# Seven-product tiles four tiles earlier in one feed-forward and two earlier in another, and scores with the other sign

## The chip, the cores and the metric

The kernel runs on one core of a Trainium2 chip. The metric is device time in microseconds (us) of one execution; lower is better. The core has a matrix engine (PE, with its weight loads shown as PEld), three engines for elementwise work (DVE, ACT, POOL) and one that issues the transfers (SP). Each has a queue of its own; they meet through semaphores.

## The reference

A two-layer decoder trunk on 1024 positions of width 1024, all in float32.

- Layer 0: a causal convolution module (norm, 1024 to 2048 matmul, gating, a depthwise convolution of 31 taps, layer norm, silu, 1024 to 1024 matmul) added to the stream, then a feed-forward.
- Then keys and values for three attention branches (compressed, selected, window) are projected once.
- Layer 1: attention of 16 heads over the three branches, gated and summed, then a feed-forward. A final norm ends it.

```
gate, up = split(rmsnorm(x) @ w_in)          # 1024 -> 2 x 2816
x = x + (silu(gate) * up) @ w_out            # 2816 -> 1024
s = where(valid, (q . k) * scale - slope * dist, -1e30);   p = softmax(s)
```

With 1024 positions and 16 blocks of 64, every block is selected, so the selected branch is full causal attention.

## The kernel before

**Staging.** Columns are positions; the 1024 positions are two halves of 512 (c = 0, 1). The kernel does layer 0 for half 0, then half 1 behind it, and so on; there are four feed-forwards, called as `ffn(layer, half)` in the order (0,0), (0,1), (1,0), (1,1). While the first runs, the convolution and the layer norm of half 1 run beside it. While (0,1) and (1,0) run, the attention of a half runs beside them. The last one, (1,1), has the final norm of half 0 beside it.

**Precision.** Each float32 operand is split into a high part (ACT copies it to fp32r) and a low part (the rest, a subtraction on DVE or POOL), and a product is three matmuls: high by high, high by low, low by high.

**A feed-forward** has 22 hidden tiles of 128 rows, j = 0 to 21 (tile 8 is the ninth). In a plain tile (`ffn_gu`) the gate and the up product are 8 blocks x 3 = 24 matmuls of 512 columns each, 48 in all (L137). After them DVE multiplies gate by up (L583), ACT takes the high part (L592) and DVE the low part (L593). After some tiles PE does a part of the second product, "the outs": 8 output tiles, each a sum over a few hidden tiles, added to the stream by DVE (L606). Which tiles go together is in `PARTS`; for (0,0) the parts start at tiles 0, 4, 8, 12, 16, 19, and the outs of a part come right after the first tile of the next.

**A seven-product tile** (`ffn_gu7`, `weights7`, `mm7`) does the 2x2 block product of (gate, up) by (first, second 256 columns) with seven block products in place of eight: 7 x 4 blocks x 3 = 84 matmuls of 256 columns (L507). `mm7` runs the products in the order 1, 2, 6, 5, 7, 3, 4. Its operands need sums:

- of the weights, for each tile: four sums on DVE (L479 to L482), seven high parts on ACT (L491), five low parts on POOL and two on DVE (L492);
- of the results: L522, L526, L527, L531 and two gating products, L561 and L562, on DVE;
- of the activations, once per feed-forward (`blocks7`, `blocks`): four groups k = 0 to 3. Each has two adds (L286), two subtractions on DVE (L439, L440) and two on POOL (L441, L442), two high parts on ACT (L452) and a low part on DVE and one on POOL (L453). Products 5 and 6 read the DVE half, products 7 and 4 the POOL half, products 1, 2 and 3 the plain activations. Every product runs over all four groups.

`ffn` takes `seven`, the first tile that is done so: `N7 = 12` for (0,0), `NREG = 4` for (1,1); the other two have none. The groups are emitted behind earlier tiles:

```
for j in range(*p):
    yield from (self.ffn_gu7 if j >= seven else self.ffn_gu)(l, j, c)
    if seven < FT and seven - 3 <= j < seven:
        self.mark(self.last)
        next(y7, None)
        next(y7, None)
```

Each `next` makes one group. `mark` and `later` hold the adds of a group (L286) in DVE's queue behind the last instruction of tile j (L593). So groups 0 and 1 stand behind tile max(seven - 3, 0), groups 2 and 3 behind the next tile.

**What sets the order.** PE's order is the order of the program text. A background generator (the convolution, the attention) is advanced by a rate per microsecond of PE work. DVE, ACT, POOL and SP get their order at build time from a list scheduler with its own time model, within data and buffer dependences. On the chip each queue runs in that order.

**The background of (0,0)**, for each of 8 tiles: DVE does 21 taps (L322, L332), POOL 9 (L329), DVE joins them (L336) and adds to a running sum (L343). Then PE spreads the sum (L382), DVE centres (8 x L385), ACT squares and DVE adds seven times (L190); PE sums that (L201), DVE takes the root, PE spreads it (L220).

**The scores** (`scores`): PE makes q.k, a DVE instruction adds the distance term and keeps the row maximum (L987), DVE negates the maximum (L993), ACT takes exp with it as bias and sums the row (L995), DVE inverts the sum (L997), POOL scales (L1000). The distance table is written once (`bias_base`); q is scaled in `q_tile`.

Of the kernel before, what the change touches and what calls it, by code (L numbers as in the profile page):

```python
# [22 lines left out]
AF = mybir.ActivationFunctionType  # L23
OP = mybir.AluOpType
# [7 lines left out]
HG = 8  # L32
DH = 64
# [1 line left out]
FH = 2816  # L35
FT = FH // 128
EPS = 1e-6
NEG = -1e30
LC = 32
NCMP = 63  # L40
SLC0 = 64
# [14 lines left out]
        (1, 0): (4, 8, 12, 15, 18), (1, 1): (4, 8, 12, 16, 19)}  # L56
PARTS = {k: list(zip((0,) + v, v + (FT,))) for k, v in CUTS.items()}
RSTD1 = 4.0
N7 = 12
PRE = 1  # L60
RAWB = (1, 2)
LNP = (), (1, 4, 6)
# [14 lines left out]
SLOPE = [2.0 ** (-8.0 * (h + 1) / NH) for h in range(NH)]  # L77
# [12 lines left out]
PP = 4  # L90
YE = 23
WX = 3
NREG = 4
FIN0 = 60.0
H = T // 2
WB = 4
# [6 lines left out]
class Net:  # L103
# [724 lines left out]
    def q_tile(self, j, c):  # L828
        nc = self.nc
        w = self.wload(self.wq[j], 8)  # L830
        ps = self.mm_ps()
        yield from self.mm3(ps, w, self.y[c], range(KT))
        for g in range(2):
            a = slice(g * DH, (g + 1) * DH)
            b = slice((1 - g) * DH, (2 - g) * DH)
            f = DH ** -0.5 / SLOPE[g * HG + j]
            q = self.tmp("q", F32R)
            nc.scalar.activation(q[a], ps[a], AF.Copy, scale=f)
            nc.vector.scalar_tensor_tensor(q[b], ps[a], f, q[a].bitcast(F32),
                                           OP.mult, OP.subtract)  # L840
            qd = self.dram.tile([128, T], F32, name=f"qd{g}_{j}_{c}")
            nc.sync.dma_start(qd, q.bitcast(F32))
            self.qd[g, j, c] = qd
# [58 lines left out]
    def bias_base(self):  # L902

        nc = self.nc
        b = self.base
        for (c0, w, step, off) in ((0, S, 1, 896), (BT_WIN, 640, 1, 512),
                                   (BT_CMP, 119, 16, 896 - (LC - 1))):
            nc.gpsimd.iota(b[:, c0:c0 + w], pattern=[[step, w]], base=-off,
                           channel_multiplier=-1, allow_small_or_imprecise_dtypes=True)
            nc.gpsimd.affine_select(out=b[:, c0:c0 + w], in_=b[:, c0:c0 + w],  # L910
                                    pattern=[[-step, w]], compare_op=OP.is_ge, fill=NEG,
                                    base=off, channel_multiplier=1)
        nc.gpsimd.affine_select(out=b[:, BT_WIN:BT_WIN + 640], in_=b[:, BT_WIN:BT_WIN + 640],
                                pattern=[[1, 640]], compare_op=OP.is_ge, fill=NEG,
                                base=-1, channel_multiplier=-1)

    def load_group(self, c, g):
# [31 lines left out]
    def scores(self, out, K, q, g, head, i, win):  # L949


        nc = self.nc
        ql = (i % 4) * 128
        mx = self.sm.tile([128, 8], F32, name="mx", tag="mx", bufs=10)
        sm = self.sm.tile([128, 2], F32, name="sm", tag="sm", bufs=10)
        if win:
            n = 128 * min(i + 1, 5)
            P = self.Pp.tile([128, 640], F32, name="PW", tag="PW", bufs=6)
            key0 = 128 * max(i - 4, 0)
            segs = [(2, 0, n, BT_WIN + 128 * max(4 - i, 0))]  # L960
        else:
            nv = NCMP if i >= 4 else NCMP // 2
            n = 64 + 128 * (i + 1)
            P = self.Pp.tile([128, 64 + S], F32, name="PS", tag="PS", bufs=5)
            key0 = 0
            segs = [(0, 0, nv, BT_CMP + 8 * (7 - i)), (1, 64, n - 64, 128 * (7 - i))]
        out[i] = P
        m = -(-n // T)
        w = -(-n // (m * 32)) * 32
        prev, spare = {}, 2  # L970
        for a in range(m):
            k0, k1 = a * w, min((a + 1) * w, n)
            ps = self.psc.tile([128, T], F32, name="sc", tag="sc", bufs=3)
            for e, k in enumerate(K[win]):
                nc.tensor.matmul(ps[:, :k1 - k0], q[:, ql:ql + 128], k[:, key0 + k0:key0 + k1],  # L975
                                 start=e == 0, stop=e == 1)
            for e, (br, p0, pn, b0) in enumerate(segs):
                s0, s1 = max(p0, k0), min(p0 + pn, k1)
                if s0 >= s1:
                    continue  # L980
                col = e
                if s1 < p0 + pn:
                    col = spare
                    spare += 1
                init = mx[:, prev[e]:prev[e] + 1] if e in prev else -3.0e38
                prev[e] = col
                nc.vector.tensor_tensor_reduce(  # L987
                    P[:, s0:s1], ps[:, s0 - k0:s1 - k0], self.base[:, b0 + s0 - p0:b0 + s1 - p0],
                    SLOPE[head], init, OP.add, OP.max, mx[:, col:col + 1])
            if a < m - 1:  # L990
                yield 2 * MM * (k1 - k0) / T
        ns = len(segs)
        nc.vector.tensor_scalar(mx[:, :ns], mx[:, :ns], -1.0, None, OP.mult)  # L993
        for e, (br, p0, pn, b0) in enumerate(segs):
            nc.scalar.activation(P[:, p0:p0 + pn], P[:, p0:p0 + pn], AF.Exp,  # L995
                                 bias=mx[:, e:e + 1], accum_out=sm[:, e:e + 1])
        nc.vector.reciprocal(sm[:, :ns], sm[:, :ns])  # L997
        for e, (br, p0, pn, b0) in enumerate(segs):
            gt = br * NH + head
            nc.gpsimd.tensor_scalar(P[:, p0:p0 + pn], P[:, p0:p0 + pn], sm[:, e:e + 1],  # L1000
                                    self.gates[:, i, gt:gt + 1], OP.mult, OP.mult)
        yield 2 * MM * (k1 - k0) / T
# [201 lines left out]
    def go(self, main, time=1e9):  # L1204


        if main is None:
            return False
        while time > 0:
            x = next(main, None)  # L1210
            if x is None:
                return False
            time -= x
            if self.bg is not None:
                self.owed += x * self.rate
                while self.owed > 0:
                    y = next(self.bg, None)
                    if y is None:
                        self.bg = None
                        break  # L1220
                    self.owed -= y
        return True
# [11 lines left out]
    def run(self):  # L1234
# [144 lines left out]
        go(fill)  # L1379
        go(self.ffn(0, 0, N7, True))  # L1380
        self.rest()
# [95 lines left out]
        self.silu = True  # L1477
        g = self.ffn(1, 1, NREG, True)
        go(g, FIN0)
# [62 lines left out]
```

## Time and profile before

| | |
|---|---|
| median of 3 runs | 2625.26 us (2624.68 to 2629.07) |
| the profiled execution | 2629.18 us |
| its span, first to last instruction | 2627.5 us |
| instructions | 37191 |
| PE busy | 2512.0 us (96%) |
| DVE busy | 1765.8 us (67%) |
| POOL busy | 1469.2 us (56%) |
| ACT busy | 1291.6 us (49%) |

The profile lists each instruction with its line, its engine, its tiles and its start; idle time in front of an instruction is put down to what released it. Matmuls overlap in the listing: the distance between two starts is what one costs. The stretches that matter here are 380 to 510 us (the first feed-forward with the convolution of half 1 beside it), 850 to 1345 and 1500 to 2150 us (the two attentions), and 2237 us to the end (the last feed-forward).

### The profile page before, as it was taken

The page shows a single profiled execution, that of the slowest core. Times are in us where ns is not written, and L with a number is a line of the kernel's source. Part 1 is how long each engine was busy: PE and PEld are TensorE (multiplying, and loading weights), DVE is VectorE, ACT ScalarE, POOL GpSimd, SP SyncE. Part 2 cuts the span into 40 slices and gives each one's busy share as a digit, 9 for nine tenths or more (in the row PEclk, how much of TensorE's full clock was granted, in tenths as well). Part 3 has the DMA queues.
Part 4 walks back from the last instruction along what each step waited for, and adds up shares of the span by engine and source line. Part 5 has one row for each costly group of instructions (what it writes and reads, how often), then busy time and mean ns, then how long its engine had stood idle before and what let it go on. Part 6 is the DMA issues. An engine that isn't in the chain of part 4 may idle for free. (4 is left out here: it accounts for less than half of the span.)

```text
span 2627.5 us, 37191 instructions
## 1 busy us (share of the span) xinstructions
PE 2512.0 (96%) x12946; PEld 2083.5 (79%) x12946; DVE 1765.8 (67%) x3652; ACT 1291.6 (49%) x2517; POOL 1469.2 (56%) x1156
## 2 busy tenths in 40 slices
PE   8898899999799999999999999999999999899997
PEld 6676788888677878887878788888888887698986
DVE  6995788677774556665556566667666655777775
ACT  6555554444534554555543355555555543334444
POOL 8794889666543554555543354535445433566664
PEclk9999899999899999999999999999999999999999
DMA  4222223232446222322355531213212124143332
GB/s 163 72 73 66 80 81 97 88 93 92 152 146 190 87 89 62 112 86 82 90 161 167 190 101 45 81 44 108 70 53 74 54 78 158 58 129 97 97 95 75
DMA packets 111212, 258.29 MB, mean 98 GB/s; under 512 B 17265, under 2 KB 28848, under 8 KB 111024
## 3 DMA queue, kind: packets, MB, share of 16 engines
q1 hardware_dynamic: 111024, 255.91, 31.0%
q8 instruction: 102, 1.67, 0.3%
q14 instruction: 86, 0.70, 0.1%
HBM read 226.37 MB, written 29.42 MB: 97 GB/s over the span
## 5 line engine op out<-in xcount | busy, mean ns | idle before, releaser
L160 POOL TENSOR_TENSOR wl<-wr,wh 128x1024 fp32r<-128x1024 f32 (+2 forms) x396 | 740.6, 1872 | 661.1 <-ACT wh L158 625.1
L137 PE MATMUL mm<-yh,wh 128*128 128x512 f32 x1424 | 595.4, 418 | 31.7 <-DVE yl L179 30.4
L137 PE MATMUL mm<-yl,wh 128*128 128x512 f32 x1424 | 567.6, 399 | 5.0 <-DVE yl L179 5.0
L137 PE MATMUL mm<-yh,wl 128*128 128x512 f32 x1424 | 566.2, 398 | 1.8 <-POOL wl L160 1.8
L158 ACT ACTIVATE wh<-wr 128x1024 fp32r<-128x1024 f32 (+2 forms) x396 | 332.5, 840 | 426.3 <-PE mm L137 287.1
L137 PE MATMUL mm<-gh,wh 128*128 128x512 f32 x1360 | 439.4, 404 | 1.8 <-ACT gh L592 1.4
L137 PEld LDWEIGHTS mm<-yh,wh 128*128 128x128 f32 x1424 | 272.1, 191 | 86.3 <-DVE yl L179 32.1
L137 PEld LDWEIGHTS mm<-yh,wl 128*128 128x128 f32 x1424 | 271.3, 191 | 63.5 <-POOL wl L160 2.2
L137 PEld LDWEIGHTS mm<-yl,wh 128*128 128x128 f32 x1424 | 272.6, 191 | 49.5 <-DVE yl L179 6.2
L1030 DVE TENSOR_TENSOR pl<-pt,ph 128x512 fp32r<-128x512 f32 (+3 forms) x320 | 206.4, 646 | 149.6 <-ACT ph L1029 148.7
L137 PEld LDWEIGHTS mm<-gh,wh 128*128 128x128 f32 x1360 | 243.3, 189 | 48.8 <-issue 3.5
L137 PE MATMUL mm<-gh,wl 128*128 128x512 f32 x680 | 270.0, 397 | 3.7 <-POOL wl L160 3.7
L1029 ACT ACTIVATE ph<-pt 128x512 fp32r<-128x512 f32 (+3 forms) x320 | 178.7, 559 | 177.6 <-PE pt L1026 175.2
L1000 POOL TENSOR_SCALAR PS<-PS,sm,gates 128x31 f32<-128x31 f32 (+9 forms) x256 | 154.7, 615 | 191.4 <-DVE sm L997 164.6
L332 DVE SCALAR_TENSOR_TENSOR mm<-u,vec,mm 128x512 f32<-128x512 f32 x306 | 225.6, 752 | 8.0 <-PE mm L320 1.8
L995 ACT ACTIVATE PS<-PS,mx 128x31 f32<-128x31 f32 (+9 forms) x256 | 139.5, 546 | 115.6 <-DVE mx L993 115.3
L329 POOL TENSOR_TENSOR zb<-zb,cv 128x512 f32<-128x512 f32 x132 | 178.8, 1355 | 14.4 <-ACT zb L314 8.8
L1000 POOL TENSOR_SCALAR PW<-PW,sm,gates 128x640 f32<-128x640 f32 (+4 forms) x128 | 96.2, 752 | 155.1 <-DVE sm L997 131.8
L606 DVE TENSOR_TENSOR h<-mm,h 128x512 f32<-128x512 f32 x184 | 124.7, 684 | 81.7 <-PE mm L137 81.3
L137 PEld LDWEIGHTS mm<-gh,wl 128*128 128x128 f32 x680 | 128.0, 188 | 37.7 <-POOL wl L160 7.5
L995 ACT ACTIVATE PW<-PW,mx 128x640 f32<-128x640 f32 (+4 forms) x128 | 88.8, 694 | 101.2 <-DVE mx L993 100.5
L507 PE MATMUL mm<-y,wh 128*128 128x256 f32 x1008 | 133.8, 286 | 2.3 <-DVE wh L492 1.9
(243 smaller groups left out, 4814.4 us busy)
## 6 DMA issues: line engine op xcount, KB each, us to landing
wr<-in_fin_dram SPq DMA_DIRECT2D x176, 512.0 KB, 3.3
wr<-in_fout_dram SPq DMA_DIRECT2D x128, 256.0 KB, 2.7
wr<-in_pw_dram SPq DMA_DIRECT2D x46, 512.0 KB, 3.3
wr<-in_fout_dram SPq DMA_DIRECT2D x64, 192.0 KB, 2.4
wr<-in_wq_dram SPq DMA_DIRECT2D x16, 512.0 KB, 4.0
qd<-q SPq DMA_DIRECT2D x32, 256.0 KB, 2.2
qt<-qd SPq DMA_DIRECT2D x32, 256.0 KB, 2.8
wr<-in_wo_dram SPq DMA_DIRECT2D x16, 512.0 KB, 3.7
```

Source lines behind the costliest of these rows:

```text
L137: nc.tensor.matmul(ps, x[:, a, :], y_, start=start and a + b == 0, stop=stop and a == n - 1 and b == 2)
L158: nc.scalar.activation(wh[:, :kt, :cols], wr[:, :kt, :cols], AF.Copy)
L160: e.tensor_tensor(wl[:, :kt, :cols], wr[:, :kt, :cols], wh[:, :kt, :cols].bitcast(F32), OP.subtract)
L329: nc.gpsimd.tensor_tensor(zb, zb, t, OP.add)
L332: later(nc.vector.scalar_tensor_tensor(ps, u[:, w:w + T], dw(w), ps, OP.mult, OP.add))
L507: nc.tensor.matmul(ps, u[:, a], v, start=a + b == 0, stop=a == n - 1 and b == 2)
L606: self.nc.vector.tensor_tensor(h, ps, h, OP.add)
L995: nc.scalar.activation(P[:, p0:p0 + pn], P[:, p0:p0 + pn], AF.Exp, bias=mx[:, e:e + 1], accum_out=sm[:, e:e + 1])
L1000: nc.gpsimd.tensor_scalar(P[:, p0:p0 + pn], P[:, p0:p0 + pn], sm[:, e:e + 1], self.gates[:, i, gt:gt + 1], OP.mult, OP.mult)
L1029: nc.scalar.activation(ph[:rows, :width], pt[:rows, :width], AF.Copy)
L1030: nc.vector.tensor_tensor(pl[:rows, :width], pt[:rows, :width], ph[:rows, :width].bitcast(F32), OP.subtract)
```

## The change

Two constants and one sign.

- `N7` goes from 12 to 8: in (0,0) tiles 8 to 11 become seven-product tiles; groups 0 and 1 now stand behind tile 5, groups 2 and 3 behind tile 6.
- `NREG` goes from 4 to 2: in (1,1) tiles 2 and 3 become seven-product tiles; groups 0 and 1 stand behind tile 0, groups 2 and 3 behind tile 1.
- q is scaled with the other sign, the distance table has the other sign, the row maximum becomes a row minimum, exp gets scale -1, and the 256 negations (L993) are gone. An added empty line moves the line numbers from there on by one, until the removed line moves them back.

```
-NEG = -1e30
+FAR = 1e30
-N7 = 12
+N7 = 8
-NREG = 4
+NREG = 2
...
-            f = DH ** -0.5 / SLOPE[g * HG + j]
+            f = -DH ** -0.5 / SLOPE[g * HG + j]
...
-            nc.gpsimd.iota(b[:, c0:c0 + w], pattern=[[step, w]], base=-off,
-                           channel_multiplier=-1, allow_small_or_imprecise_dtypes=True)
+            nc.gpsimd.iota(b[:, c0:c0 + w], pattern=[[-step, w]], base=off,
+                           channel_multiplier=1, allow_small_or_imprecise_dtypes=True)
...
-                init = mx[:, prev[e]:prev[e] + 1] if e in prev else -3.0e38
+                init = mx[:, prev[e]:prev[e] + 1] if e in prev else 3.0e38
...
-                    SLOPE[head], init, OP.add, OP.max, mx[:, col:col + 1])
+                    SLOPE[head], init, OP.add, OP.min, mx[:, col:col + 1])
...
-        nc.vector.tensor_scalar(mx[:, :ns], mx[:, :ns], -1.0, None, OP.mult)
...
-            nc.scalar.activation(P[:, p0:p0 + pn], P[:, p0:p0 + pn], AF.Exp,
+            nc.scalar.activation(P[:, p0:p0 + pn], P[:, p0:p0 + pn], AF.Exp, scale=-1.0,
                                  bias=mx[:, e:e + 1], accum_out=sm[:, e:e + 1])
```

PE's order is the same in both programs but for the converted tiles and the place of the background's few matmuls among them.

**DVE in the last feed-forward**, before, around the last group and the first seven-product tile (`wh` and `ws` are weights, `et`, `y` the activation sums, `g`, `gh` the hidden tile, `u` the first result of a seven-product tile):

```order
L440 TENSOR_TENSOR et<-yt,et 128x256
L480 TENSOR_TENSOR ws<-ws,wr 128x512
L481 TENSOR_TENSOR ws<-wr 128x512
L453 TENSOR_TENSOR y_22231<-et,y_22230 128x512
L439 TENSOR_TENSOR et<-yt 128x256
L440 TENSOR_TENSOR et<-yt,et 128x256
L482 TENSOR_TENSOR ws<-wr,ws 128x512
L453 TENSOR_TENSOR y_22249<-et,y_22248 128x512
L583 SCALAR_TENSOR_TENSOR mm<-mm,sg 128x512
L492 TENSOR_TENSOR wh<-wr,wh 128x512
L593 TENSOR_TENSOR gh<-mm,gh 128x512
L522 TENSOR_TENSOR u<-mm,et 128x512
```

and after the change:

```order
L583 SCALAR_TENSOR_TENSOR mm<-mm,sg 128x512
L492 TENSOR_TENSOR wh<-wr,wh 128x512
L593 TENSOR_TENSOR gh<-mm,gh 128x512
L286 TENSOR_TENSOR yt<-yh,yl 128x512 x4
L439 TENSOR_TENSOR et<-yt 128x256
L440 TENSOR_TENSOR et<-yt,et 128x256
L453 TENSOR_TENSOR y_22186<-et,y_22185 128x512
L439 TENSOR_TENSOR et<-yt 128x256
L440 TENSOR_TENSOR et<-yt,et 128x256
L479 TENSOR_TENSOR ws<-wr 128x512
L453 TENSOR_TENSOR y_22204<-et,y_22203 128x512
L522 TENSOR_TENSOR u<-mm,et 128x512
```

Before, the low part of group 3 (the second L453) is followed by the end of a whole plain tile (L583, L593) ahead of the first seven-product result (L522). After, the last plain tile (L583, L593) stands ahead of groups 2 and 3, and L522 right behind them.

**DVE in the first feed-forward**, before, around the end of the convolution and its centring (`z`, `acc`: the convolution; `h`: the outs):

```order
L332 SCALAR_TENSOR_TENSOR mm<-u,vec,mm 128x512 x2
L606 TENSOR_TENSOR h_94<-mm,h_94 128x512
L332 SCALAR_TENSOR_TENSOR mm<-u,vec,mm 128x512
L606 TENSOR_TENSOR h_95<-mm,h_95 128x512
L606 TENSOR_TENSOR h_96<-mm,h_96 128x512
L606 TENSOR_TENSOR h_97<-mm,h_97 128x512
L336 TENSOR_TENSOR z<-mm,zb 128x512
L343 TENSOR_TENSOR acc<-acc,z 128x512
L606 TENSOR_TENSOR h_98<-mm,h_98 128x512
L606 TENSOR_TENSOR h_99<-mm,h_99 128x512
L606 TENSOR_TENSOR h_100<-mm,h_100 128x512
L385 SCALAR_TENSOR_TENSOR z<-mm,z 128x512 x8
```

and after:

```order
L593 TENSOR_TENSOR gh<-et,gh 128x512
L336 TENSOR_TENSOR z<-mm,zb 128x512
L482 TENSOR_TENSOR ws<-wr,ws 128x512
L606 TENSOR_TENSOR h_99<-mm,h_99 128x512
L479 TENSOR_TENSOR ws<-wr 128x512
L343 TENSOR_TENSOR acc<-acc,z 128x512
L606 TENSOR_TENSOR h_100<-mm,h_100 128x512
L492 TENSOR_TENSOR wh<-wr,wh 128x512
L480 TENSOR_TENSOR ws<-ws,wr 128x512
L481 TENSOR_TENSOR ws<-wr 128x512
L385 SCALAR_TENSOR_TENSOR z<-mm,z 128x512 x8
L482 TENSOR_TENSOR ws<-wr,ws 128x512
```

Before, only outs (L606) stand around the last steps of the convolution (L336, L343). After, weight sums and low parts of seven-product tiles (L479 to L482, L492) stand between them and behind them, ahead of the centring (L385).

**DVE in the first feed-forward, groups 2 and 3**: before,

```order
L286 TENSOR_TENSOR yt<-yh,yl 128x512 x2
L439 TENSOR_TENSOR et<-yt 128x256
L286 TENSOR_TENSOR yt<-yh,yl 128x512
L440 TENSOR_TENSOR et<-yt,et 128x256
L286 TENSOR_TENSOR yt<-yh,yl 128x512
L453 TENSOR_TENSOR y_4004<-et,y_4003 128x512
L439 TENSOR_TENSOR et<-yt 128x256
L440 TENSOR_TENSOR et<-yt,et 128x256
L453 TENSOR_TENSOR y_4022<-et,y_4021 128x512
L583 SCALAR_TENSOR_TENSOR mm<-mm,sg 128x512
```

and after:

```order
L439 TENSOR_TENSOR et<-yt 128x256
L332 SCALAR_TENSOR_TENSOR mm<-u,vec,mm 128x512
L440 TENSOR_TENSOR et<-yt,et 128x256
L332 SCALAR_TENSOR_TENSOR mm<-u,vec,mm 128x512 x2
L453 TENSOR_TENSOR y_3451<-et,y_3450 128x512
L286 TENSOR_TENSOR yt<-yh,yl 128x512
L332 SCALAR_TENSOR_TENSOR mm<-u,vec,mm 128x512
L286 TENSOR_TENSOR yt<-yh,yl 128x512
L439 TENSOR_TENSOR et<-yt 128x256
L440 TENSOR_TENSOR et<-yt,et 128x256
L583 SCALAR_TENSOR_TENSOR mm<-mm,sg 128x512
L453 TENSOR_TENSOR y_3469<-et,y_3468 128x512
```

Before, the groups follow each other with no taps between; after, convolution taps (L332) stand between their steps, and the end of tile 7 (L583) ahead of the last low part.

## Rows read from the trace of the kernel before

**Rows 1.** Page, busy us, share of the span and instructions of each engine.
```profile
PE 2512.0 (96%) x12946; PEld 2083.5 (79%) x12946; DVE 1765.8 (67%) x3652; ACT 1291.6 (49%) x2517; POOL 1469.2 (56%) x1156
```

**Rows 2.** Windows; busy us (count) of PE, PEld, DVE, ACT, POOL, granted clock, DMA share, GB/s.
```profile
400.00:450.00 50.00, 50.00 (x221) 41.20 (x220) 45.78 (x63) 27.23 (x40) 47.12 (x33) 1.00 0.26 80
408.36:476.46 68.10, 68.10 (x297) 55.51 (x296) 56.72 (x75) 35.17 (x52) 57.54 (x38) 1.00 0.31 97
530.99:575.50 44.51, 42.38 (x338) 40.75 (x337) 38.29 (x47) 19.80 (x40) 29.57 (x21) 1.00 0.29 90
2328.72:2369.00 40.28, 40.28 (x339) 40.23 (x338) 34.31 (x47) 18.03 (x36) 26.99 (x17) 1.00 0.33 110
```

**Rows 3.** Timeline of PE, first feed-forward; start, us, engine, line, operation [idle <-releaser].
```profile
440.72 0.63 PE L137 MATMUL mm<-gh,wh 128*128 128x512 f32 x2
...
463.14 1.02 PE L382 MATMUL mm<-acc,ones 128*128 128x512 f32 x2
...
479.23 0.28 PE L201 MATMUL mm<-ones,acc 128*128 128x1 f32 x2
...
498.54 0.28 PE L507 MATMUL mm<-yh,wh 128*128 128x256 f32 x1
...
508.62 0.63 PE L137 MATMUL mm<-gh,wh 128*128 128x512 f32 x2
```

**Rows 4.** Timeline of DVE, first feed-forward.
```profile
408.36 0.70 DVE L583 SCALAR_TENSOR_TENSOR mm<-mm,sg 128x512 f32<-128x512 f32 x1 [0.51 <-PE mm L137]
...
430.12 0.70 DVE L583 SCALAR_TENSOR_TENSOR mm<-mm,sg 128x512 f32<-128x512 f32 x1 [0.97 <-PE mm L137]
```

**Rows 5.** Lines by form, DVE, 380 to 700 us; count | busy us, mean ns | idle, releaser.
```profile
L332 DVE SCALAR_TENSOR_TENSOR mm<-u,vec,mm 128x512 f32<-128x512 f32 x62 | 46.5, 752 | 1.4
...
L286 DVE TENSOR_TENSOR yt<-yh,yl 128x512 f32<-128x512 f32 x8 | 7.1, 908 | 0.0
...
L453 DVE TENSOR_TENSOR y<-et,y 128x512 fp32r<-128x512 f32 x4 | 3.5, 886 | 1.2 <-ACT y L452 1.0
...
L440 DVE TENSOR_TENSOR et<-yt,et 128x256 f32<-128x256 f32 x4 | 2.5, 630 | 0.0
...
L439 DVE TENSOR_TENSOR et<-yt 128x256 f32<-128x256 f32 x4 | 1.6, 412 | 0.0
```

**Rows 6.** Timeline of DVE, last feed-forward.
```profile
2255.58 0.70 DVE L583 SCALAR_TENSOR_TENSOR mm<-mm,sg 128x512 f32<-128x512 f32 x1 [5.94 <-PE mm L137]
...
2266.78 0.70 DVE L583 SCALAR_TENSOR_TENSOR mm<-mm,sg 128x512 f32<-128x512 f32 x1 [9.14 <-PE mm L137]
...
2281.03 0.68 DVE L583 SCALAR_TENSOR_TENSOR mm<-mm,sg 128x512 f32<-128x512 f32 x1
...
2283.41 3.72 DVE L286 TENSOR_TENSOR yt<-yh,yl 128x512 f32<-128x512 f32 x4
...
2291.18 1.78 DVE L453 TENSOR_TENSOR y<-et,y 128x512 fp32r<-128x512 f32 x1
...
2295.93 1.04 DVE L453 TENSOR_TENSOR y<-et,y 128x512 fp32r<-128x512 f32 x1
```

**Rows 7.** Waits of PE, 2230 to 2628 us; us, times, longest.
```profile
PE mm L507 <- ACT y L452: 2.4, 1, 2.4
...
PE mm L507 <- DVE y L453: 1.0, 2, 0.7
```

**Rows 8.** Timeline of PE, last feed-forward.
```profile
2297.43 4.46 PE L507 MATMUL mm<-y,wh 128*128 128x256 f32 x24
```

**Rows 9.** Waits of PE, first attention, 850 to 1345 us.
```profile
PE pt L1026 <- POOL PS L1000: 2.3, 4, 1.5
```

**Rows 10.** Waits of PE, second attention, 1500 to 2150 us.
```profile
PE po L1051 <- DVE pl L1030: 2.8, 8, 0.7
PE po L1051 <- ACT ph L1029: 1.9, 2, 1.3
```

**Rows 11.** Lines, DVE, whole span.
```profile
L993 DVE TENSOR_SCALAR mx<-mx 128x1 f32<-128x1 f32 (+1 forms) x256 | 81.0, 319 | 3.5
```

More of the change, by code (lines that the diff above doesn't have):

```diff
@@ L907, in bias_base @@
                                    (BT_CMP, 119, 16, 896 - (LC - 1))):
-            nc.gpsimd.iota(b[:, c0:c0 + w], pattern=[[step, w]], base=-off,
-                           channel_multiplier=-1, allow_small_or_imprecise_dtypes=True)
+            nc.gpsimd.iota(b[:, c0:c0 + w], pattern=[[-step, w]], base=off,
+                           channel_multiplier=1, allow_small_or_imprecise_dtypes=True)
             nc.gpsimd.affine_select(out=b[:, c0:c0 + w], in_=b[:, c0:c0 + w],
-                                    pattern=[[-step, w]], compare_op=OP.is_ge, fill=NEG,
+                                    pattern=[[-step, w]], compare_op=OP.is_ge, fill=FAR,
                                     base=off, channel_multiplier=1)
         nc.gpsimd.affine_select(out=b[:, BT_WIN:BT_WIN + 640], in_=b[:, BT_WIN:BT_WIN + 640],
-                                pattern=[[1, 640]], compare_op=OP.is_ge, fill=NEG,
+                                pattern=[[1, 640]], compare_op=OP.is_ge, fill=FAR,
                                 base=-1, channel_multiplier=-1)
```

## The prediction

> **What bounds the kernel now.** I read the page first: PE is busy 96% of the span [rows 1], so a gain must come from less PE work or from the waits that are left, and a loss from new waits of PE. Next the windows around the edits. Between 400 and 450 us PE never stops, but DVE is busy 45.8 of 50 us and POOL 47.1 [rows 2]: the convolution of half 1 runs there, and it is where four tiles are to change kind. In the attentions PE's waits are single microseconds [rows 9, 10]. In the last feed-forward the waits view names the activation sums (L452, L453) as something that PE already waits for, 2.4 + 1.0 = 3.4 us [rows 7].
>
> **What a converted tile gives.** A plain tile: two tile ends are seen by DVE at 408.36 and 430.12 with PE as the releaser, so 21.76 / 2 = 10.88 us [rows 4]; in the last feed-forward 2255.58 to 2266.78, 11.20 us [rows 6]. A seven-product tile: 498.54 to 508.62, 84 matmuls in 10.08 us, 0.12 each [rows 3]. Four in a row take 44.51 us (11.1 each) in the first feed-forward and 40.28 (10.1 each) in the last [rows 2]. So 10.88 - 10.08 = 0.8 us at best for each of four tiles, nothing if they go as the four in a row did, and 1.1 us for each of two: at most 3.2 + 2.2 = 5.4 us less PE time.
>
> A rule that speaks against it is in the Trainium skill, "TensorE: Matmul & The Clock Gate", section "Part 3: Packing small matmuls — row/col tiling": a weight load overlaps running matmuls only where the row groups differ. All loads here fill the whole array, so by that page's figures load and 256 columns would cost 107 + 109 = 216 ns (an estimate), 18 us a tile and over 40 us more for six. The rows show 0.12 us for the pair, so the load is hidden; the measurement decides, and the sum goes by it.
>
> **What it adds on DVE.** In the four tiles in a row DVE is busy 38.29 us, 9.6 a tile, and POOL 29.57, 7.4 a tile [rows 2]. The groups cost DVE, by the means of one, 8 x 0.908 + 4 x 0.886 + 4 x 0.63 + 4 x 0.412 = 15 us [rows 5]. In the first feed-forward both now fall where DVE has a few microseconds free in 50.
>
> **First feed-forward, the waits in order.** Up to tile 5 the queues are unchanged. Tile 8 starts at 440.72 - 10.88 = 429.84 [rows 3, 4]. Products 1 and 2 need no group: 24 x 0.12 = 2.9, then product 6 reads group k from 432.7 on, group 3 at 433.8. In the new DVE order the low part of group 3 comes after tile 5's L583 (408.36 [rows 4]) and, counted in that order, 20 taps (15.0 us [rows 5]), the groups (15 us) and ten others, at a tap's 0.75 at least 7.5: 37.5 us, so 446; consecutive instructions overlap by a little, so 443 to 448. **PE stands some 12 us in tile 8.**
>
> Then the centring. Its place in PE's order is nine products into tile 9, and L201 follows 133 products later, 142 products behind the outs. With no wait PE would be at L201 at 429.84 + 10.08 + 22.42 (the outs, 440.72 to 463.14 [rows 3]) + 142 x 0.12 = 479.4. DVE must have done the seven sums of L190 by then. Before, DVE was busy 56.72 us between 408.36 and the last of them at 476.46 [rows 2]. Now, in the same part of its queue, it has also: five taps that stood before 408.36 (3.8), the groups (15), and from the order 7 low parts, 13 weight sums and little more than one tile's results, together 2.5 of a tile's load (2.5 x 9.6 = 24); two plain tile ends (2 x 1.4) are gone. 56.7 + 3.8 + 15 + 24 - 2.8 = 96.7: **DVE can't be through before 408.4 + 96.7 = 505.1**, if it never idles. Adding the instructions one by one without overlap gives 514. I take 508, nearer to the window's row. So PE loses 508 - 479.4 = 29 us over tile 8, L382 and L201 together. What is left to the end of tile 12 is 193 products, 23.2 us: 531, where it was 508.62 [rows 3]. **+23 us** (+20 to +29), the gain of the four tiles already in it. If DVE had idle time for this, it would cost nothing; it had 68.1 - 56.7 = 11.4 us [rows 2], which I have used up. POOL's share of this (7.4 a tile, and half of the groups) lies beside it and is not later by my count; if it is, the end goes up.
>
> **Last feed-forward.** Now groups 2 and 3 stand right in front of the tile that needs them. Tile 1 ends at 2266.78, and tile 2 is at product 6 2.9 us later; it reads group 3 at 2270.7. Before, the second pair was preceded by a tile end at 2281.03, its adds began at 2283.41 and its last low part ended at 2295.93 + 1.04 = 2296.97 [rows 6]: 15.9 us from L583. In the new order the first pair has that pattern (weight sums between) behind tile 0's end, 2255.58 [rows 6]: it ends at 2271.5. DVE is in order, so tile 1's L583 and L593 wait behind it, and the second pair's adds begin 2.4 later, 2273.9. From adds to the last low part 2296.97 - 2283.41 = 13.6 with weight sums between; the new order has one (L479), so about 12.5: 2286.4. **PE waits 15.7 us** where it waited 3.4. The slow pace behind such a wait is there already: the 24 matmuls behind the 3.4 us took 4.46 us where 24 x 0.12 is 2.9 [rows 8, 3]. Net 15.7 - 3.4 - 2.2 = **+10 us**. From below: if the whole new pair took what its first half took before (2291.18 + 1.78 - 2283.41 = 9.5 [rows 6]), +7; from above, a late weight transfer in front of L479, +13.
>
> **The score sign.** 256 instructions of 0.319 us, 81 us of DVE, go [rows 11]. PE waits 2.3 us in the first attention for POOL's scaling, and 2.8 and 1.9 in the second for DVE's and ACT's halves of the weights [rows 9, 10]: no more than 7.0 can come back. L993 stood in the chain to the scaling and in front of L1030 in DVE's queue; I take 2.5. The minimum, the sign in exp's scale and the other table replace operations of the same size one for one; no row shows a row minimum. From below it gives nothing; were it slower, DVE, which is idle for a third of the span [rows 1], has room for it: 0.
>
> **Sum.** +23 + 10 - 2.5 = +30.5 on the profiled 2629.18, 2659.7. That execution is 3.9 us above the median of the runs, so on the median's level **2656 us**, +1.2%.
>
> **Rivals.**
>
> - The tail is absorbed: PE loses the 12 us of tile 8, less 3.2 for its shorter tiles, and DVE is in time for L382 and L201, because it works on while PE does the outs (22.4 us); the last feed-forward is as above. +9 + 10 - 2.5: 2642. For it: those outs need little of DVE. Against it: 96.7 us of work stand in 71 us.
> - Faster: the sums are there in time in both places, because DVE's instructions run shorter than these means, which were taken beside a busy POOL. It decides at two points: group 3 at 433.8 instead of 446 and at 2270.7 instead of 2286.4. Then nothing waits, the 3.4 us go too: -5.4 - 3.4 - 2.5, 2614. Against it: DVE would need 25 us in place of 37.5, and the last feed-forward's pattern was measured where POOL was half idle.
> - Worse: taps, groups and the results of a tile take their scratch from one ring of five buffers. Before, the convolution had ended when seven-product tiles began; now ACT may stand at a scratch tile for POOL's taps, and with it the high parts of the weights, at tile 8 and at each of 9 to 11. Two more 12 us waits: 2680. No row shows such a wait, as the two never met.
> - The change does less than it says: no, the order has 84-matmul tiles in all six places.
>
> **How the numbers follow.** Forecast 0.62 (its own range 2646 to 2667), absorbed tail 0.17, worse 0.13, faster 0.08. Below 0.2% (5.3 us) a run can't be told from no change. The range takes in the absorbed tail with its last feed-forward at +7 (2639) and the worse case, with a few microseconds beyond both: 2636 to 2686. Faster 0.08; within 0.2%, a mixture of faster and absorbed, 0.03; slower 0.89.
>
> **What would show it.** PE: an idle of 9 to 14 us in tile 8 put down to L453 or L452, then idle at L382 and L201, and tile 12 ending near 531; an idle near 15 us about 2270, put down to L453; attention waits of 7 us falling. Wrong, if tile 12 ends before 515, or if the waits of tile 2 of the last feed-forward stay under 8 us.

## The result, and the profile after

The changed kernel takes 2650.38 us (median of 4 runs, 2648.56 to 2652.69) where the kernel before took 2627.16 beside it (4 runs): ratio 1.009, 95% interval 1.0077 to 1.0102. It is slower by 0.9%, about 23 us; the prediction was 2656, in a range from 2636 to 2686. The profiled execution took 2648.56 us, its span 2646.9 us.

The busy times on the changed kernel's page are these:

```profile
PE 2507.1 (95%) x13162; PEld 2096.9 (79%) x13162; DVE 1752.8 (66%) x3462; ACT 1317.5 (50%) x2559; POOL 1480.3 (56%) x1174
```

Against [rows 1] PE is busy 4.9 us less and the span is 19.4 us longer, so by these records PE is idle 24.3 us more. Where that lies is read from four windows, with the same places of PE's work as borders: start of tile 8, start of the outs, L382, L201, end of tile 12. The columns are: stretch, its length, busy time (and instructions) of PE, PEld, DVE, ACT and POOL, granted clock, DMA share, GB/s.

```profile
428.24:459.64 31.40, 13.19 (x85) 12.11 (x84) 27.59 (x38) 15.16 (x26) 26.79 (x22) 0.67 0.11 30
459.64:487.64 28.00, 23.67 (x108) 19.08 (x106) 26.52 (x38) 11.49 (x19) 23.72 (x18) 0.97 0.32 98
487.64:512.42 24.78, 19.46 (x136) 18.22 (x136) 23.21 (x30) 12.00 (x22) 12.97 (x9) 0.84 0.24 75
512.42:543.01 30.59, 28.81 (x204) 28.16 (x205) 19.92 (x40) 12.96 (x25) 12.10 (x9) 0.87 0.20 61
```

Before, the same stretches took 10.88 us (a plain tile), 22.42, 16.09 and 29.39 by [rows 3, 4]. So tile 8 costs 20.5 us more, the way to L382 5.6, the way to L201 8.7, the rest 1.2: 36 us, and 34.4 at the end of tile 12 (543.01 for 508.62), since this execution was 1.6 us ahead at tile 8. DVE is nearly full in the first three. Ahead of the first attention (758.89 us before, 787.13 after) some 6 us of it have come back. In this stretch PE's waits at L201 fell from 5.0 to 3.3 us, and those of L507 for POOL's low parts from 3.1 to 1.7.

PE's waits in these windows are (us in all, times, longest):

```profile
PE mm L507 <- ACT y L452: 17.0, 2, 12.8
PE mm L201 <- DVE acc L190: 5.3, 1, 5.3
PE mm L382 <- DVE acc L343: 4.3, 1, 4.3
PE mm L220 <- DVE dg L213: 1.8, 1, 1.8
PE mm L507 <- DVE y L453: 1.1, 1, 1.1
```

L507 behind L452 and L453 is tile 8: 18 us. Then come L382, L201 and L220; the rows of L382 and L201 before have no idle time [rows 3].

In the last feed-forward PE's timeline (start, length, instruction, and in brackets the idle time before it) has the new waits in tile 2, which starts at 2276.81:

```profile
2280.44 0.38 PE L507 MATMUL mm<-y,wl 128*128 128x256 f32 x1 [0.29 <-ACT y L452]
2281.51 0.51 PE L507 MATMUL mm<-y,wl 128*128 128x256 f32 x2 [0.69 <-DVE y L453]
2291.09 1.52 PE L507 MATMUL mm<-y,wl 128*128 128x256 f32 x3 [9.07 <-ACT y L452]
2294.22 0.58 PE L507 MATMUL mm<-y,wl 128*128 128x256 f32 x1 [1.61 <-ACT y L452]
2295.82 0.80 PE L507 MATMUL mm<-y,wl 128*128 128x256 f32 x2 [1.02 <-DVE y L453]
```

They sum to 12.7 us, where [rows 7] had 3.4. From that point to tile 0 of the last feed-forward (2236.73 before, 2246.04 after), where both attentions lie, the delay shrank from 28.2 to 9.3 us: PE went this way 19 us quicker. That is far more than the 7.0 us of waits that stood in the attentions before [rows 9, 10].

### The profile page after: what moved, and what is told of

The parts are those of the page before. It is cut to its first block, busy times and chain, and to the rows that moved or that the text cites. A ratio compares the mean times of both kernels' runs of the same rounds, so it can differ in the third digit from the quotient of the medians.

```text
span 2646.9 us, 37558 instructions
## 1 busy us (share of the span) xinstructions
PE 2507.1 (95%) x13162; PEld 2096.9 (79%) x13162; DVE 1752.8 (66%) x3462; ACT 1317.5 (50%) x2559; POOL 1480.3 (56%) x1174
## 4 chain that ended last, share of the span: by engine, by line
PE 74%; DVE 11%; POOL 4%; DMA 4%; issue 3%; ACT 3%; SPq 0%; DVEq 0%; ACTq 0%; POOLq 0%
PE mm L137 49%; PE mm L507 7%; PE po L1051 6%; PE sc L976 5%; PE pt L1026 5%; POOL wl L160 2%; DMA wr<-in_fin_dram 1%; DMA wr<-in_fout_dram 1%; DVE acc L190 1%; POOL zb L329 1%; DVE yt L272 1%; ACT wh L158 1%; DVE yl L179 1%; DVE mm L332 1%; DVE wh L492 1%
## 5 line engine op out<-in xcount | busy, mean ns | idle before, releaser
L160 POOL TENSOR_TENSOR wl<-wr,wh 128x1024 fp32r<-128x1024 f32 (+2 forms) x384 | 708.5, 1846 | 646.1 <-ACT wh L158 606.8
L137 PE MATMUL mm<-yh,wh 128*128 128x512 f32 x1328 | 558.0, 420 | 32.5 <-DVE yl L179 29.8
L137 PE MATMUL mm<-yl,wh 128*128 128x512 f32 x1328 | 529.7, 399 | 4.2 <-DVE yl L179 4.2
L137 PE MATMUL mm<-yh,wl 128*128 128x512 f32 x1328 | 529.2, 399 | 1.8 <-POOL wl L160 1.8
L158 ACT ACTIVATE wh<-wr 128x1024 fp32r<-128x1024 f32 (+2 forms) x384 | 319.9, 833 | 383.3 <-PE mm L137 250.8
L137 PEld LDWEIGHTS mm<-yh,wh 128*128 128x128 f32 x1328 | 254.7, 192 | 83.0 <-DVE yl L179 31.5
L137 PEld LDWEIGHTS mm<-yh,wl 128*128 128x128 f32 x1328 | 253.4, 191 | 59.6 <-POOL wl L160 2.2
L137 PEld LDWEIGHTS mm<-yl,wh 128*128 128x128 f32 x1328 | 255.1, 192 | 45.4 <-DVE yl L179 5.8
L332 DVE SCALAR_TENSOR_TENSOR mm<-u,vec,mm 128x512 f32<-128x512 f32 x306 | 225.7, 753 | 6.9 <-PE mm L320 0.8
L606 DVE TENSOR_TENSOR h<-mm,h 128x512 f32<-128x512 f32 x184 | 124.9, 685 | 79.5 <-PE mm L137 79.0
L507 PE MATMUL mm<-y,wh 128*128 128x256 f32 x1224 | 165.7, 289 | 2.4 <-DVE wh L492 2.3
L507 PEld LDWEIGHTS mm<-y,wh 128*128 128x128 f32 x1224 | 157.3, 197 | 4.4 <-DVE wh L492 3.8
```

The costliest lines, as they stand in the source:

```text
L137: nc.tensor.matmul(ps, x[:, a, :], y_, start=start and a + b == 0, stop=stop and a == n - 1 and b == 2)
L158: nc.scalar.activation(wh[:, :kt, :cols], wr[:, :kt, :cols], AF.Copy)
L160: e.tensor_tensor(wl[:, :kt, :cols], wr[:, :kt, :cols], wh[:, :kt, :cols].bitcast(F32), OP.subtract)
L332: later(nc.vector.scalar_tensor_tensor(ps, u[:, w:w + T], dw(w), ps, OP.mult, OP.add))
L507: nc.tensor.matmul(ps, u[:, a], v, start=a + b == 0, stop=a == n - 1 and b == 2)
```

## Experiments

**The parts one at a time.** E1 to E3 do one part of the change each, on the kernel before. Each expectation names its theories (A, B, C) with the times that they would give; what stands behind it says which of them held. A number in brackets behind a ratio is its 95% interval.

E1, the sign alone: `N7 = 12` and `NREG = 4` put back in the changed kernel.

> Only the score sign of the change: seven-product tiles stay at the 13th and the 5th. Theory A (the three parts act apart from each other, each at its place): the negations are gone from both attentions and nothing else moves, so this is faster than the kernel before by what the attentions gained in the changed kernel, 4.7 us in the first, 4.1 behind it and 8.7 in the second, 12 to 18 us in all (my prediction had 2.5). Rival B (most of that gain belongs to the later start of the stages behind the long first feed-forward, whose waits had been shifted, not to the sign): 2 to 8 us faster. Rival C (the sign gives nothing): within 2 us.

It takes 2611.17 us against 2626.37 for the kernel before, ratio 0.994 (0.9927 to 0.9952): 15.2 us faster. Theory A holds.

E2, the first feed-forward alone:

```
-N7 = 12
+N7 = 8
```

> Only the first feed-forward of the change: seven-product tiles from the 9th, the last one and the sign as before. Theory A: slower by 28 to 31 us, the whole of what the trace shows at the end of that stage and the norm behind it, with 18 us of waits in the 9th tile and the half pace to the 13th. Rival B: part is given back later by waits that were there anyway (POOL's normalisation of half 1), so 18 to 25 us slower; my prediction's term was 23. Rival C (the groups' lateness is an effect of all parts together): under 15 us.

It takes 2656.26 us against 2626.37, ratio 1.0111 (1.0096 to 1.0126): 29.9 us slower, with an interval from 25.2 to 33.1 us. Theory A holds. Its waits are those of the changed kernel (L507 behind L452 17.0, L201 5.3, L382 4.1).

E3, the last feed-forward alone:

```
-NREG = 4
+NREG = 2
```

> Only the last feed-forward of the change: seven-product tiles from its 3rd, the rest as before. Theory A: 9 to 12 us slower, with about 12 us of waits in its 3rd tile where 3.4 were. Rival B (the end of the program hides part, since the final norm of half 0 beside it keeps POOL and DVE busy and PE has to wait for these anyway): 3 to 7 us slower. Rival C: no change within 2 us.

It takes 2634.01 us against 2626.37, ratio 1.0025 (1.0015 to 1.0035): 7.6 us slower, between the ranges of A and B; the interval, 3.9 to 9.2 us, reaches into both. The stage itself is 9.0 us longer (from tile 0's L583 to the outs after tile 4, 58.0 for 49.0 us). The three parts sum to -15.2 + 29.9 + 7.6 = 22.3 us, and all together cost 23.2: within the intervals they act apart from each other.

**What in the sign gives 15 us.** E4 is E1 with a multiplication by 1.0 where the negation stood; each engine then has the order of the kernel before. The line that it adds is

```
+        nc.vector.tensor_scalar(mx[:, :ns], mx[:, :ns], 1.0, None, OP.mult)
```

> The score sign turned, with a multiplication by 1.0 put where the negation stood: every engine has the order of the kernel before, with the minimum in place of the maximum and the sign inside exp. Theory A (what the sign part gives is the one instruction less in the chain from scores to weights): the time of the kernel before, within 2 us. Rival B (the minimum or exp with a scale is itself quicker or slower): off by more than 4 us, up to the whole gain of 12 to 18.

It takes 2627.0 us against 2626.37, ratio 1.0002 (0.9993 to 1.0011). Theory A holds: minimum for maximum and the scale in exp cost and give nothing, and the removed instruction gives the whole 15 us. E5 keeps such an instruction too, but lets it write a tile of its own that nobody reads (`...` marks what is left out):

```
+        dm = self.sm.tile([128, 2], F32, name="dm", tag="dm", bufs=2)
...
+        nc.vector.tensor_scalar(dm[:, :ns], mx[:, :ns], 1.0, None, OP.mult)
```

> The score sign turned as in e1, and beside it 256 instructions of the size of the old negation are kept on DVE, which write a tile that nobody reads: DVE's queue is as long as before, but no instruction stands between the row's minimum and exp. Theory A (the gain of 15 us comes from the shorter chain from scores to weights): 12 to 16 us faster, as e1. Rival B (it comes from DVE's 81 us less, which let PE's other halves of weights come sooner): within 3 us of the kernel before. Something between, 5 to 9 us faster, would say that both count.

It takes 2612.66 us against 2627.29, ratio 0.9939 (0.9925 to 0.9952): 14.6 us faster, as theory A says. The second attention as one window reads, in E4, E1 and E5 in this order:

```profile
1491.13:2160.42 669.29, 663.97 (x3511) 555.04 (x3510) 441.06 (x1285) 372.01 (x761) 313.03 (x284) 1.00 0.24 72
```

```profile
1482.49:2142.61 660.12, 659.62 (x3511) 555.90 (x3510) 410.49 (x1157) 376.70 (x761) 312.46 (x284) 1.00 0.24 73
```

```profile
1483.16:2144.66 661.50, 659.84 (x3511) 555.74 (x3510) 437.17 (x1285) 376.69 (x761) 311.93 (x284) 1.00 0.24 73
```

DVE does 1285 instructions in E4 and in E5, and E5 is 7.8 us shorter all the same: what counts is that exp no longer stands behind the instruction, not DVE's time. (The list scheduler also gives E1 and E5 an order of DVE that differs a little from E4's; its share was not measured apart.) And PE's *busy* time is 4.1 us less in E5 than in E4 at the same 3511 matmuls and the same granted clock, so the idle time (5.3 us in E4) does not show all that the late weights cost. The matmuls that read those weights (`pl`, `ph`) are these by line over this window, in E4 and then in E1 (busy, mean ns of one | idle before):

```profile
L1051 PE MATMUL po<-ph,V 128*128 128x512 f32 (+3 forms) x256 | 85.3, 336 | 2.0 <-ACT ph L1029 1.9
L1051 PE MATMUL po<-pl,V 128*128 128x512 f32 (+3 forms) x256 | 83.0, 346 | 3.0 <-DVE pl L1030 2.9
```

```profile
L1051 PE MATMUL po<-ph,V 128*128 128x512 f32 (+3 forms) x256 | 85.1, 335 | 0.0
L1051 PE MATMUL po<-pl,V 128*128 128x512 f32 (+3 forms) x256 | 81.7, 341 | 0.4 <-DVE pl L1030 0.4
```

PE's timeline in E4 shows how a wait hides:

```profile
1938.47 0.40 PE L137 MATMUL mm<-yl,wh 128*128 128x512 f32 x1
1938.70 0.40 PE L137 MATMUL mm<-yh,wl 128*128 128x512 f32 x1
1938.94 0.34 PE L1051 MATMUL po<-ph,V 128*128 128x384 f32 x1
1940.08 0.45 PE L1051 MATMUL po<-pl,V 128*128 128x384 f32 x1 [0.80 <-DVE pl L1030]
```

In such rows a matmul of 512 columns is 0.40 us long and the next starts 0.23 us after it, so a delay of less than the difference shows no idle time. Counted from the start of the matmul before to their own start, the L1051 matmuls of the window take 111.3 us in E4 and 103.2 in E1. These are 8.1 of the 9.2 us by which the window is shorter; the rest is spread over the other lines. The Trainium skill says in "Perfetto Trace Analysis", section "Identifying the Most-Contended Engine", that matmul busy time is not a good measure of how close a kernel is to roofline, because matmuls are pipelined. This window agrees that busy time misleads: 4.1 us of E4's went away with the waits.

The rest of E1's gain lies before that window. From 824.19 to 1490.20 us of E4, with the first attention in it, PE's waits at L1026 (2.4 us) and L1051 (0.6) are gone in E1, and the same stretch (822.17 to 1481.56) is 6.6 us shorter.

**What holds the first feed-forward.** E6 is E2 with the groups two tiles earlier:

```
-                if seven < FT and seven - 3 <= j < seven:
+                if seven < FT and seven - 5 <= j < seven:
```

> Seven-product tiles from the 9th in the first feed-forward alone, as e2 (29.9 us slower), but the four groups of activation sums are made behind the 4th and 5th tiles in place of the 6th and 7th. Theory A (DVE has more work up to L201 than it can do, wherever the groups stand): the 18 us of waits in the 9th tile go, but PE then waits as long at L382 and L201; 15 to 28 us slower than before. Rival B (only the late groups cost): 0 to 10 us slower.

It takes 2653.73 us against 2627.29, ratio 1.0097 (1.0083 to 1.011): 26.4 us slower, in theory A's range, but only in part by its mechanism. The waits at L382 and L201 did grow, to 6.3 and 8.0 us, and no wait for the groups is left. But PE still stands 13.5 us in tile 8, for another reason. These are PE, then ACT and POOL around it:

```profile
446.15 0.58 PE L507 MATMUL mm<-yh,wl 128*128 128x256 f32 x1 [13.53 <-ACT wl L491]
```

```profile
440.30 0.72 ACT L328 ACTIVATE cv<-u,vec 128x512 f32<-128x512 f32 x1 [0.74 <-POOL zb L329]
441.64 0.72 ACT L328 ACTIVATE cv<-u,vec 128x512 f32<-128x512 f32 x1 [0.62 <-POOL zb L329]
442.99 0.72 ACT L328 ACTIVATE cv<-u,vec 128x512 f32<-128x512 f32 x1 [0.62 <-POOL zb L329]
444.33 0.72 ACT L328 ACTIVATE cv<-u,vec 128x512 f32<-128x512 f32 x1 [0.63 <-POOL zb L329]
444.96 0.61 ACT L491 ACTIVATE wh<-ws 128x512 fp32r<-128x512 f32 x1
```

```profile
437.66 9.34 POOL L329 TENSOR_TENSOR zb<-zb,cv 128x512 f32<-128x512 f32 x7 [2.02 <-ACT zb L314]
```

ACT writes a product for each of POOL's taps into the scratch ring (L328) and gets a buffer back whenever POOL has added one, every 1.34 us. The high parts of tile 8's weights (L491) stand behind these in ACT's queue. That is the mechanism of the rival with the ring of five buffers, in tile 8 alone.

E7 and E8 are E2 with one queue relieved. In the last two convolution tiles of half 1, E7 leaves out DVE's taps but the first of each tile:

```
-            if w < CW:
+            if w < CW and not (c and j > 5):
```

and E8 leaves out POOL's taps with ACT's copies for them:

```
-            if w < n1:
+            if w < n1 and not (c and j > 5):
```

> As e2, but the DVE taps of the last two convolution tiles of half 1 are left out of the computation, but for the first of each: 40 instructions of 0.75 us, 30 us of DVE's queue, from about 415 us on. Theory A (DVE's queue up to L201 sets the loss): 0 to 12 us slower than before in place of 29.9. Rival B (POOL's adds, which hold the scratch ring and with it the groups, set it): 20 us slower or more.

> As e2, but POOL's taps of the last two convolution tiles of half 1 are left out of the computation, with the ACT copies that feed them: 18 adds of about 1.5 us on POOL and 18 copies of 0.7 on ACT. Theory A (DVE's queue sets the loss): 18 us slower than before or more, with the wait in the 9th tile shorter by the few microseconds in which DVE stood for POOL's adds. Rival B (POOL and the ring set it): 0 to 12 us slower.

E7 takes 2651.84 us against 2627.29, ratio 1.0091 (1.0077 to 1.0104), 24.6 us slower. E8 takes 2653.94, ratio 1.0099 (1.0084 to 1.0113), 26.7 us slower. Both intervals overlap that of E2. Theory A failed in E7, theory B in E8: neither queue is *the* cause. E7's DVE shows why, in front of group 2:

```profile
439.15 0.69 DVE L286 TENSOR_TENSOR yt<-yh,yl 128x512 f32<-128x512 f32 x1 [3.60 <-POOL zb L329]
440.99 0.69 DVE L286 TENSOR_TENSOR yt<-yh,yl 128x512 f32<-128x512 f32 x1 [1.15 <-POOL zb L329]
442.84 0.42 DVE L439 TENSOR_TENSOR et<-yt 128x256 f32<-128x256 f32 x1 [1.15 <-POOL zb L329]
```

With 30 us of its own work gone, DVE idles for scratch buffers that POOL's taps free (L286 writes one of the ring and doesn't read `zb`), and the wait in tile 8 stays at 16 us. In E8, PE's waits between 425 and 490 us are these:

```profile
PE mm L382 <- DVE acc L343: 12.8, 1, 12.8
PE mm L507 <- ACT y L452: 5.2, 2, 3.0
PE mm L507 <- DVE y L453: 3.3, 2, 2.5
```

Tile 8 is down to 8.5 us, and DVE's taps now come late for L382. E9 leaves both out:

> As e2, but both DVE's taps (but for the first of each tile) and POOL's taps of the last two convolution tiles of half 1 are left out of the computation: what e7 and e8 left out one at a time, each of which still cost 24 to 26 us. Theory A (two in-order queues, DVE's and POOL's with ACT at the scratch ring behind it, are each full in front of the 9th tile and up to L201, so that taking the load off one shows the other): with both relieved the loss falls to 0 to 12 us. Rival B (the loss lies in the order itself: groups, weights of seven-product tiles and the centring are put behind each other, whatever else runs): 18 to 25 us as in e7 and e8.

It takes 2644.22 us against 2627.81, ratio 1.0065 (1.0051 to 1.0078): 16.4 us slower, clearly less than E2. Tile 8's wait is 4.7 us and L382 is in time, but the loss is only halved, between A and B: the step from L382 to L201 is as slow as in E2 (24.9 us there). That window in E9 reads

```profile
469.70:494.95 25.25, 16.96 (x138) 16.28 (x136) 25.18 (x30) 12.20 (x24) 15.59 (x11) 0.90 0.29 94
```

DVE is busy 25.18 of 25.25 us. In the kernel before the same window, with no weight sums in it, reads

```profile
463.14:479.23 16.09, 16.09 (x70) 12.96 (x69) 14.43 (x20) 8.48 (x14) 10.31 (x4) 1.00 0.31 108
```

In E9's queue the weight sums of tiles 9 to 11 stand between the sums of squares (L190), and those with both inputs in SBUF that start while a POOL instruction runs are slow. Here is DVE in E9, and POOL beside it:

```profile
476.67 4.86 DVE L385 SCALAR_TENSOR_TENSOR z<-mm,z 128x512 f32<-128x512 f32 x8
...
482.65 0.69 DVE L492 TENSOR_TENSOR wh<-ws,wh 128x512 fp32r<-128x512 f32 x1
483.26 1.78 DVE L480 TENSOR_TENSOR ws<-ws,wr 128x512 f32<-128x512 f32 x1
484.96 0.68 DVE L190 TENSOR_TENSOR acc<-acc,sq 128x512 f32<-128x512 f32 x1
```

```profile
478.61 1.31 POOL L492 TENSOR_TENSOR wl<-wr,wl 128x512 fp32r<-128x512 f32 x1 [2.41 <-DVE z L385]
...
482.78 1.71 POOL L492 TENSOR_TENSOR wh<-ws,wh 128x512 fp32r<-128x512 f32 x1 [1.30 <-ACT wh L491]
```

L480 takes 1.78 us beside a POOL instruction, L190 0.68 right behind it with POOL idle. L385, which reads PSUM and one SBUF tile, takes 0.61 (4.86 / 8) although POOL works beside it.

E12 is E9 with the squares of the centring but the first left out, and their sums L190:

```
-            else:
+            elif j == 0:
                 self.sumsq(c, j, z[j], nc.vector)
```

> As e9 (16 us slower than before, with an idle of 8.3 us left at L201 and 3.7 at L220), and the squares of the centring but the first are left out too, with their seven sums on DVE (L190), so that the centring's work no longer stands among the weight sums of the seven-product tiles. Theory A (between L382 and L201 DVE is full: 25.2 of 25.3 us in e9, with the weight sums of three tiles among the centring's): the idle at L201 goes to under 2 us and the time is 4 to 11 us slower than before. Rival B (what is left of the loss is PE's own slow pace behind the first waits, or the weights of tiles 10 to 12, which stay late): 13 to 18 us slower, with the waits shifted to L507.

It takes 2635.11 us against 2627.3, ratio 1.0029 (1.002 to 1.0038): 7.8 us slower, as theory A says. PE's idle time at L201 is gone, and the granted clock is full in the window:

```profile
470.90:487.71 16.81, 16.81 (x138) 16.33 (x137) 16.81 (x22) 6.72 (x14) 9.89 (x8) 1.00 0.28 94
```

What is left are waits of 4.7 us in tile 8 and of 6.4 at L220, for DVE's root, which stands among the same kind of weight sums.

**The last feed-forward.** E10 is E3 with all four groups behind tile 0:

```
-                    next(y7, None)
-                    next(y7, None)
+                    for _ in range(4 if l else 2):
+                        next(y7, None)
```

> Seven-product tiles from the 3rd of the last feed-forward alone, as e3 (7.6 us slower), but all four groups of activation sums stand behind its first tile in place of two behind the first and two behind the second. Theory A (the wait in the 3rd tile comes from the place of groups 2 and 3 behind the second tile's end): the wait of 12 us falls under 5, and the time is 4 us slower than before to 4 us faster. Rival B (DVE can't do the groups and the weight sums in that stretch, wherever they stand): 5 to 9 us slower as e3.

It takes 2635.66 us against 2627.81, ratio 1.0027 (1.0015 to 1.0039): 7.85 us slower. Theory A failed, B holds. The waits are cut up, not smaller (13.1 us in all between 2250 and 2285, where E3 had 12.4):

```profile
PE mm L507 <- ACT y L452: 9.8, 3, 4.1
PE mm L507 <- DVE y L453: 3.3, 3, 2.4
```

and from tile 0's end until the last group DVE is nearly full, 28.64 of 31 us here and 28.50 of 29.50 in E3 (the second row):

```profile
2250.00:2281.00 31.00, 17.87 (x84) 14.17 (x83) 28.64 (x31) 10.53 (x19) 23.03 (x18) 0.78 0.16 51
```

```profile
2250.95:2280.45 29.50, 17.08 (x82) 13.43 (x80) 28.50 (x31) 10.30 (x19) 21.62 (x17) 0.80 0.17 54
```

PE's last wait for a group ends 30.5 us behind tile 0's L583 here (2280.36, 2249.82) and 29.7 in E3 (2280.67, 2250.95), in either place of the groups. How much of DVE's time there is its own work and how much POOL's slowing of it was not run.

E11 is E1 with the groups of the last feed-forward one tile earlier, where two plain tiles' time is left for them:

```
-                if seven < FT and seven - 3 <= j < seven:
+                if seven < FT and seven - 3 - l <= j < seven:
```

> The score sign turned (e1, 15 us faster), seven-product tiles from the 13th and the 5th as in the kernel before, and the groups of the last feed-forward made one tile earlier, behind its first and second tiles in place of the second and third. Theory A (PE's wait of 3.4 us in the 5th tile and the slow pace behind it come from the groups' place): 18 to 22 us faster than before. Rival B (the sums collide with the final norm and the residual sums at the start, so nothing is won): 13 to 16 us faster.

It takes 2604.05 us against 2627.81, ratio 0.9915 (0.9902 to 0.9929): 23.8 us faster. Theory A holds, by more than it expected: no wait for a group is left, and PE is busy throughout the stretch where E1 waits 3.2 us:

```profile
2249.00:2295.00 46.00, 46.00 (x244) 39.10 (x244) 31.44 (x41) 16.89 (x30) 30.33 (x24) 1.00 0.23 69
```

From its first seven-product matmul to the next outs E11 takes 10.0 us (2271.68 to 2281.66), E1 16.4 (2271.21 to 2287.59). This version beats both kernels.

## Why the prediction was right, step by step

The time and its direction were right, and the first feed-forward is the largest term, as forecast. But all three terms were off, two of them by much and in opposite directions, and two mechanisms were only in part what happens.

- **The converted tiles.** The hidden weight load, by which I let a tile take 84 x 0.12 us, held: E12 passes 138 matmuls in 16.81 us, 0.12 each. What the tiles gain can't be read off, since waits lie over it.
- **The wait in tile 8**, "some 12 us": 18. I counted 37.5 us of DVE's queue and came to 446 for group 3; its DVE half was ready at 452.1, POOL's at 453.5. The count of work held: DVE was busy 36.3 us of the 45.3 from tile 5's L583 to that point. What the sum lacked are the 9 us in which DVE stood, 5.2 of them for POOL's `zb` ahead of the groups. (The rows below the next point show this: the idle time first, then two windows, from that L583 to group 3's low part and to L201.) E7 shows that without the taps in that queue the wait hardly changes: scratch and POOL's taps are late as well. E9 shows that both must go.
- **L201 at 508** from 96.7 us of DVE work: 512.42, and this execution was 1.6 us ahead at tile 8, so 6 us short. Right in kind (E9, E12). The work was 92.8 us where I counted 96.7. In the other 12.9 of the 105.7 us DVE stood; my 508 had room for 3 us of that.

```profile
412.70 0.69 DVE L336 TENSOR_TENSOR z<-mm,zb 128x512 f32<-128x512 f32 x1 [5.24 <-POOL zb L329]
```

```profile
406.76:452.09 45.33, 27.18 (x130) 22.40 (x128) 36.31 (x50) 18.71 (x33) 38.06 (x30) 0.81 0.14 41
406.76:512.42 105.66, 77.80 (x421) 67.19 (x419) 92.80 (x126) 47.70 (x82) 80.39 (x61) 0.86 0.21 63
```

- **Tile 12's end at 531**: 543. The step that failed is "193 products, 23.2 us". I let PE run on at the full pace; the stretch from L201 took 30.6 us, with 1.8 us of wait and a granted clock of 0.87. Of the 34.4 us at tile 12's end some 6 came back later, which I had not in the sum. The term is 29.9 us by E2 (25.2 to 33.1) where I had 23, its range ending at 29.
- **The last feed-forward**, "+10 us" with a wait of 15.7: 12.7 us of waits, the stage 9.7 us longer by the borders of E3, and 7.6 us in all by E3. The size was nearly right, the reason was not: I put it to the place of groups 2 and 3 behind tile 1. E10 moves them without effect. What binds is all that DVE has to do between tile 0's end and the groups' use in tile 2. E11, with tile 4 as the first seven-product tile, gives such work one more tile, and the waits vanish.
- **The score sign**, -2.5: -15.2 by E1. "No more than 7.0 can come back" was the error: the idle column is not an upper bound, because matmul records are longer than their spacing (0.40 and 0.23 us). That the negation stood in the chain to the scaling was right (E4, E5).
- **The rivals.** The absorbed tail fell at L201 and L382, where DVE was late by 5.3 and 4.3 us. The faster case fell in tile 8. The ring of five buffers is real (13.5 us in tile 8 of E6, DVE's idle time in E7), but in none of these runs did it strike four times: in the changed kernel tiles 9 to 11 waited for no weights.

With the measured terms the sum is 29.9 + 7.6 - 15.2 = 22.3 us, near the measured 23.2, where I had 30.5. That 2656 came out near 2650 is in part luck: the first term was 6.9 us too low, the other two 2.4 and 12.7 too high.

What stays open: how much of E9's and E12's gain would also come to the kernel before with the same work left out (not run), and whether a larger scratch ring would help.

## What to carry to other kernels

Before work is moved to an earlier stage, add up what every in-order queue has to do between the last point where its inputs exist and the first where PE needs the result; here, moving the work within that stretch changed nothing (E10), and one tile more took the waits away (E11). When two queues are both full, relieving either one may show little gain (5 and 3 us here, of 30), so test them together too (14 us). An instruction of 0.3 us, in a chain that PE waits for many times, can be worth more than the idle time shown there: count from the start of one matmul to the start of the next.

## What the runs showed of the hardware

- DVE instructions on 128x512 with both inputs in SBUF stretch from 0.68 us to between 1.2 and 1.8 beside POOL, and POOL's from 1.30 to 1.7 (E9); in the last feed-forward four L286 took 5.74 us in E3. The Trainium skill's page "SBUF — State Buffer", section "SBUF: two separate sides", has a rule for it: a DVE instruction with two SBUF inputs and a GpSimd (POOL) instruction that reads SBUF take a shared pair of ports by an exclusive lock: the one that starts first has it to its end, and the other blocks. The rows of E9 agree: L480 ends 0.55 us behind POOL's end (485.04 and 484.49), and L385, with one input in PSUM, isn't slowed.
- In these windows PE's granted clock fell around waits: its mean is 0.67 in tile 8's window, with 18 us idle, 0.84 from L382 to L201, behind an idle of 4.3 us and with one of 5.3, and 1.00 in E12's window from L382 to L201, which has none. The levels are 1.2 and 2.4 GHz, so 0.84 means a third of the stretch at the lower one. The first two matmuls of L201 take 0.58 us there, where they took 0.28 before [rows 3].
